# 1/rms of the tokens spread over the partitions by transfers through DRAM, not by products

## The chip, the cores and the metric

One core of a Trainium2 chip (TRN2) runs the whole program in one launch. The metric is the device time of one execution in microseconds (us), the median of the runs shown. Engines: PE (TensorE, matrix products), DVE (VectorE), ACT (ScalarE), POOL (GpSimd), SP (SyncE, which issues most transfers). SBUF is the on-chip memory with 128 partitions, PSUM the one that products write to, in banks.

## The reference

One inference step of a decoder with two layers, on 512 prompt tokens and 8 sample tokens together (520 columns), model width 1024, feed-forward width 2816.

```python
def _rmsnorm(x, g):
    xf = x.astype(jnp.float32)
    y = xf * lax.rsqrt(jnp.mean(xf * xf, axis=-1, keepdims=True) + EPS)
    return (y * g.astype(jnp.float32)).astype(x.dtype)

def _swiglu(x, wg, wu, wd):
    return (jax.nn.silu(x @ wg) * (x @ wu)) @ wd
# every layer:  x += 0.5*SwiGLU(rms(x));  x += mixer(rms(x));  x += 0.5*SwiGLU(rms(x))
# mixer of layer 0: causal pooling over windows of 2, 4, 8, 16; of layer 1: sliding-window
# attention with sinks, on K and V projected once from the stream after layer 0 (_rmsnorm there too)
```

So there is a norm ahead of each of four half layers of SwiGLU, of each mixer, of K and V, and at the end. What matters here is 1/rms, one number for each token.

## The kernel before, in words

The stream is kept turned: model width on the partitions, eight tiles of 128 x 520, tokens along the free dimension. A product is fp32r: each operand is split into a high part (`xh`, `wh`, by ACT) and a low part (`xl`, `wl`, by DVE), and three products of these make one. Feed-forward tiles are made from sums and differences of inputs and of weights (`t12`, `t34`, `th`, `tl`, `S`), so that fewer products do; POOL adds one weight block to another with accumulating transfers (`S<-raw`, `raw<-raw`).

A norm doesn't scale its input. The products run on x times the gain, and 1/rms of each token multiplies the result: `g<-g,R`, `g<-ps,R`, `cs<-cs,R` on DVE. For that, `R` (128 x 520) holds 1/rms of all tokens in every partition. It comes about in two steps. First, sums of squares give 1/rms with the token on the partition, in `r_tok`: four columns for the 512 prompt tokens (token 128 t + p in row p of column t), and a fifth whose rows 112 to 119 hold the sample tokens. Then that is spread: for each column, PE multiplies the identity `ident` by the column broadcast to 128 x 128, which leaves the 128 numbers along the free dimension in all partitions, and ACT copies the bank into `R`. The products are plain fp32, and the profile counts two passes for each, ten for a norm.

This spreading stands at four places:

- place 1: the norm of the first half layer of layer 0 (`first_hooks` calls `rstd_all` between products, about 38 us into the span),
- place 2: the norm of the second half layer of layer 0 (`begin`, steps `N.b`, `N.c0`, `N.c1`, about 412 us),
- place 3: the norm for K and V (the fourth hook of `kv_pass`, about 778 us); the first reader of R here multiplies the cosine and sine tables, `cs<-cs,R`, from which `kT` comes, which PE turns at L1618,
- place 4: the norm of the last half layer (`begin` again, about 1287 us).

At places 1 and 3 `r_tok` is computed by DVE in Newton steps (L506 to L513), at 2 and 4 by POOL with a power (L805). The norms of the pooling mixer, of the attention and the last one have code of their own and aren't touched.

What sets the order: around places 2 and 4 a planner gives each engine its order of steps, from each step's cost and due time (`add(name, engine, cost, due, ...)`); an engine then takes its steps in that order. Elsewhere the order of the program, changed a little by a scheduler, stands. An engine's queue is taken strictly in order: an instruction that waits holds up what is behind it. All weight loads, and every transfer passed through `later(...)`, are issued by SP in the order of the program: `raw<-...gate`, `raw<-...up` (half a megabyte each), `S<-...up` (a quarter).

Of the kernel before, what the change touches and what calls it, by code (L numbers as in the profile page):

```python
# [11 lines left out]
F32 = mybir.dt.float32  # L12
# [6 lines left out]
P = 128  # L19
# [3 lines left out]
SP = 512  # L23
NS = 8
TOK = SP + NS
# [220 lines left out]
class Steps:  # L246
# [8 lines left out]
    def add(self, name, eng, cost, due, fn=None, after=(), takes=(), reads=()):  # L255
        self.steps[name] = (eng, cost, due, fn, tuple(after), tuple(takes))
        for key in reads:
            self.readers.setdefault(key, []).append(name)
# [58 lines left out]
def yoco_step(ctx, tc, ins, outs):  # L317
    nc = tc.nc
# [3 lines left out]
    V, S, T = nc.vector, nc.scalar, nc.tensor  # L322
# [2 lines left out]
    big = ctx.enter_context(tc.tile_pool(name="big", bufs=8))  # L325
    rawp = ctx.enter_context(tc.tile_pool(name="rawp", bufs=3))
    splp = ctx.enter_context(tc.tile_pool(name="splp", bufs=6))
    psum = ctx.enter_context(ExitStack())
    banks_ = []

# [33 lines left out]
    def later(ins):  # L364

        return tc.keep_in_program_order(ins)
# [87 lines left out]
    ident = cp.tile([P, P], F32, name="ident")  # L454
# [14 lines left out]
    r_tok = cp.tile([P, 8], F32, name="r_tok")  # L469
    R = cp.tile([P, TOK], F32, name="R")  # L470
# [18 lines left out]
    pss_ = [None]  # L489
# [22 lines left out]
            o = r_tok[:, :5] if it == 2 else y  # L512
            V.scalar_tensor_tensor(o, t1, 1.5, y, op0=ALU.add, op1=ALU.mult)  # L513

    def rstd_all():

        pr, pr2 = pss_[0][:, 1, :], pss_[0][:, 0, 8 : 8 + NS]
        for t in range(4):
            T.matmul(
                pr[:, t * P : (t + 1) * P], r_tok[:, t : t + 1].broadcast_to([P, P]), ident, start=True, stop=True  # L520
            )
        T.matmul(pr2, r_tok[:, 4:5].broadcast_to([P, P]), ident[:, 112:120], start=True, stop=True)
        S.copy(R[:, :SP], pr)
        S.copy(R[:, SP:], pr2)


    def terms(w, xx):
        return ((w[0], xx[0]), (w[0], xx[1]), (w[1], xx[0]))
# [256 lines left out]
    def begin(st, fi, n, mov, tmp, tt, first, off, base, need, ready, summed, hidden_list, root_):  # L785


        add, vals = st.add, {}
# [15 lines left out]
        def n_root():  # L804
            nc.gpsimd.tensor_tensor(r_tok[:, :5], vals["v"], minus_half, op=ALU.pow)  # L805

        def n_spread():
            pr, pr2 = pss_[0][:, 1, :], pss_[0][:, 0, 8 : 8 + NS]
            for t in range(4):
                T.matmul(  # L810
                    pr[:, t * P : (t + 1) * P], r_tok[:, t : t + 1].broadcast_to([P, P]), ident, start=True, stop=True
                )
            T.matmul(pr2, r_tok[:, 4:5].broadcast_to([P, P]), ident[:, 112:120], start=True, stop=True)

        def n_copy(a):
            if a == 0:
                S.copy(R[:, :SP], pss_[0][:, 1, :])
            else:
                S.copy(R[:, SP:], pss_[0][:, 0, 8 : 8 + NS])

        d = base + root_
        add("N.s", "PE", 0.62, d, n_sums, after=summed, takes=("d",))
        add("N.m", "DVE", 0.17, d, n_mean, after=["N.s"])
        add("N.r", "POOL", 1.4, d, n_root, after=["N.m"])
        add("N.b", "PE", 1.0, d, n_spread, after=["N.r"])
        add("N.c0", "ACT", 0.6, d, lambda: n_copy(0), after=["N.b"])
        add("N.c1", "ACT", 0.18, d, lambda: n_copy(1), after=["N.c0"], reads=[("d", "N.s")])

        def scaled(k, a):
            vals["X", k, a] = z = tmp.tile([P, TOK], F32, tag="sa", name="xab"[:1] + "ab"[a])  # L830
# [23 lines left out]
        for k in range(4):  # L854
            d = S0 - 14.0 + 3.0 * k
# [30 lines left out]
        for p in range(npl):  # L886
# [4 lines left out]
            for q, (k, o) in enumerate(order):  # L891
                i = off + 4 * p + 2 * (k // 4) + o
                after = [f"wl{i}"] + need(k) + ([prev] if prev else [f"p{p - 1}.71"] if p else [])
# [5 lines left out]
            d = P0(p + 1)  # L899
# [4 lines left out]
                reads=[("d", f"p{p}.01"), ("t", f"S{p}")],  # L904
# [103 lines left out]
    with ff_pool() as tmp:  # L1008
# [29 lines left out]
        with tc.tile_pool(name="st", bufs=1, space=bass.MemoryType.PSUM, reuse_waits="tile") as stp:  # L1038
            st = Steps(dict(t=3, m=1, w=6, sq=4))
            add = st.add  # L1040
# [94 lines left out]
            for k in range(KT):  # L1135
                d = T0 + UP * k
                add(
                    f"t{k}", "PE", 0.45, d, lambda k=k: turn_x(k),
                    after=["i"] + [f"x{k // 2}.{c}" for c in range(2)] + ([f"t{k - 1}"] if k else []), takes=("t",),
# [4 lines left out]
                for e, lo, hi, cost in pieces:  # L1144
                    add(
                        f"c{k}{e}", e, cost, d + 0.5, lambda k=k, e=e, lo=lo, hi=hi: copy_x(k, e, lo, hi),
                        after=[f"t{k}"] + (["tab"] if e == "ACT" else []), reads=[("t", f"t{k}")],
# [5 lines left out]
                for o in range(2):  # L1153
# [3 lines left out]
                        after=[f"e{k}", f"wl{w}"] + ([f"p{k - 1}{o}"] if k else []),  # L1157
                        reads=[("w", f"wh{w}")] if k % 4 == 3 else [],
# [5 lines left out]
                    after=[f"q{k}"] + ([f"a{k - 1}"] if k else []), reads=[("sq", f"q{k}")],  # L1164
                )
            for i in range(8):
                d = (6.0, 6.6, 11.5, 12.2, 19.0, 20.5, 22.0, 23.5)[i]
                add(
                    f"wh{i}", "ACT", 0.63, d, lambda i=i: w_hi(i),
                    after=[f"w{i if i < 4 else 7}"] + ([f"wh{i - 1}"] if i else []), takes=("w",),  # L1170
# [104 lines left out]
    with ff_pool() as tmp:  # L1275
# [3 lines left out]
        add = st.add  # L1279
# [165 lines left out]
        for m in (6, 7):  # L1445
            d = 4.35 * (m - 6)
            for h in range(2):
# [13 lines left out]
                after=[f"q{m}", "x5" if m == 6 else "a6"], reads=[("sq", f"q{m}")],  # L1461
# [15 lines left out]
        for gi in range(4):  # L1477
            ready = [f"{k}{2 * gi + i}" for k in ("l", "sl") for i in range(2)] if gi == 3 else ["x5"]
            for tau in (0, 1, 2, 3, 4):
                d = Z_DUE[gi] + 0.72 * tau  # L1480
                add(
                    f"z{gi}{tau}", "PE", 0.71, d + (3.0 if tau == 4 and gi == 0 else 3.5 if tau == 4 and gi == 2 else 0), lambda gi=gi, tau=tau: z_part(gi, tau),
                    after=ready + ([f"z{gi}0"] if tau else []) + (["ns"] if tau == 4 and gi < 2 else [])
# [8 lines left out]
                    after=[f"z{gi}{tau}", "nr" if tau < 4 else "n5"] + ([f"eh{gi}0"] if tau else []),  # L1492
# [5 lines left out]
                    after=[f"eh{gi}{tau}"] + last, reads=[("d", holder)],  # L1498
# [3 lines left out]
        for m in range(KT):  # L1502
            gi, d = m // 2, B_DUE(m)
            need = ((0, 1), (1, 2, 3), (4,))
            for part in range(3):
                add(
                    f"b{m}{part}", "PE", (0.6, 0.72, 0.22)[part], d + 0.1 * part, lambda m=m, part=part: band(m, part),
                    after=[f"ez{gi}{t}" for t in need[part]] + ([f"b{m}0"] if part else [f"b{m - 1}0"] if m else []),
# [4 lines left out]
                reads=[("d", f"b{m}0")],  # L1513
# [6 lines left out]
                reads=[("sq", f"sq{m}")],  # L1520
# [147 lines left out]
    with tc.tile_pool(name="at", bufs=2) as at, tc.tile_pool(  # L1668
        name="pat", bufs=2, space=bass.MemoryType.PSUM, reuse_waits="tile"
# [34 lines left out]
        add = st.add  # L1704
# [191 lines left out]
        for t in range(KT):  # L1896
            d = q_due(t)
# [144 lines left out]
        for g in range(2):  # L2042
            d = S_DUE[g]
# [364 lines left out]
```

## Time and profile before

| what | value |
|---|---|
| median of 3 runs | 1651.93 us (1651.38 to 1654.89) |
| profiled execution | 1651.43 us, span 1649.7 us |
| granted TensorE clock | 0.998 |
| PE, DVE, ACT, POOL busy | 1635.1, 1241.2, 877.0, 178.2 us |
| moved by DMA | 226.28 MB, mean 137 GB/s |
| DMA packets | 317423, of them 9520 under 512 B |

The profile's times are in us from the start of the span. A row of the timeline is: start, duration, engine, line, operation, out<-in, shape, count, and in brackets how long the engine had been idle before and what ended that. Products overlap in the pipeline, so a row's duration is longer than the distance to the next start. "L519" is line 519 of the kernel before. A row of the windows gives, for a stretch of time, the busy time of each engine with its count of instructions, then the granted clock, the mean share of the 16 DMA engines that were busy (it can go a little over 1), and the GB/s that they moved.

### The profile page before, as it was taken

To read this page: it belongs to the slowest core of one execution; us is meant where nothing else is said; L and a number is where in the kernel's file an instruction comes from. 1 tells how busy PE (TensorE), PEld (TensorE's weight loads), DVE (VectorE), ACT (ScalarE), POOL (GpSimd) and SP (SyncE) were. 2 spreads that over 40 slices of the span, in tenths; PEclk is the share of its full clock that TensorE was granted. 3 is DMA by queue.
4 is the path that set the end of the run, shared out by engine and by line. 5 is a ranking of instruction groups with operands and counts; after the bars stand their busy time and mean duration, and the time that the engine had idled before them with its cause. 6 is when DMAs were issued, how large, how long until landed. Compare 5 with 4: busy or idle time off the path is not lost.

```text
span 1649.7 us, 34525 instructions
## 1 busy us (share of the span) xinstructions
PE 1635.1 (99%) x13814; PEld 1620.5 (98%) x13814; DVE 1241.2 (75%) x2351; ACT 877.0 (53%) x1756; POOL 178.2 (11%) x236
## 2 busy tenths in 40 slices
PE   9999999999999999999999999999999999999997
PEld 9999999999999999999999999999989999999997
DVE  7966875878775875878784785778997785785786
ACT  6643643666652652556562552555875662563463
POOL 1101101001101101100201101100220110110100
PEclk9999999999999999999999999999999999999999
DMA  9546845761655765633756665654142566665641
GB/s 244 135 120 136 175 141 137 164 204 54 149 153 134 167 160 135 154 109 97 169 153 155 131 165 152 139 150 114 27 104 65 129 154 166 140 156 149 128 121 52
DMA packets 317423, 226.28 MB, mean 137 GB/s; under 512 B 9520, under 2 KB 292776, under 8 KB 317222
## 3 DMA queue, kind: packets, MB, share of 16 engines
q1 hardware_dynamic: 290832, 178.24, 38.7%
q0 software_dynamic: 23104, 41.31, 15.9%
q10 hardware_dynamic: 3326, 4.53, 0.9%
q8 instruction: 108, 1.77, 0.4%
q14 instruction: 53, 0.43, 0.1%
HBM read 180.63 MB, written 5.04 MB: 113 GB/s over the span
## 4 chain that ended last, share of the span: by engine, by line
PE 97%; DVE 1%; ACT 0%; DMA 0%; issue 0%; SPq 0%; DVEq 0%; ACTq 0%
PE ps L560 48%; PE ps L534 36%; PE pa L534 5%; PE ps L2203 2%; PE ps L1378 1%; PE pb L1808 1%; PE p L534 1%; PE pc L1879 1%; PE pc L1864 1%; PE ps L1415 1%; DMA raw<-in_ffn_w_gate_dram 0%; PE ps L2244 0%; DVE wl L225 0%; PE t L1066 0%; DVE sm L1827 0%; PE ps L498 0%
## 5 line engine op out<-in xcount | busy, mean ns | idle before, releaser
L195 ACT ACTIVATE wh<-raw 128x512 fp32r<-128x512 f32 (+1 forms) x658 | 397.9, 622 | 482.2 <-PE ps L534 285.8
L196 DVE TENSOR_TENSOR wl<-raw,wh 128x512 fp32r<-128x512 f32 (+1 forms) x658 | 434.8, 677 | 176.3 <-ACT wh L195 172.7
L560 PE MATMUL ps<-th,wh 128*128 128x260 f32 x1248 | 352.1, 283 | 1.0 <-DVE sb L653 0.8
L560 PE MATMUL ps<-tl,wh 128*128 128x260 f32 x1248 | 352.4, 282 | 0.0
L560 PE MATMUL ps<-th,wl 128*128 128x260 f32 x1248 | 350.9, 282 | 0.0
L560 PEld LDWEIGHTS ps<-th,wh 128*128 128x128 f32 x1248 | 234.5, 188 | 1.5 <-DVE sb L653 1.0
L560 PEld LDWEIGHTS ps<-tl,wh 128*128 128x128 f32 x1248 | 234.7, 188 | 0.0
L560 PEld LDWEIGHTS ps<-th,wl 128*128 128x128 f32 x1248 | 234.3, 188 | 0.0
L534 PE MATMUL ps<-hh,wh 128*128 128x260 f32 x1024 | 206.5, 283 | 0.6 <-ACT vtok L1630 0.6
L534 PE MATMUL ps<-hl,wh 128*128 128x260 f32 x1024 | 207.0, 282 | 0.0
L534 PE MATMUL ps<-hh,wl 128*128 128x260 f32 x1024 | 205.1, 282 | 0.0
L560 PE MATMUL ps<-xh,wh 128*128 128x260 f32 x696 | 195.0, 282 | 0.6 <-ACT sb L643 0.6
L560 PE MATMUL ps<-xl,wh 128*128 128x260 f32 x696 | 194.9, 282 | 0.0
L560 PE MATMUL ps<-xh,wl 128*128 128x260 f32 x696 | 191.6, 282 | 0.0
L158 POOL DMA_DIRECT2D raw<-raw x78 | 69.2, 887 | 1068.8 <-DVE wl L196 446.0
L534 PEld LDWEIGHTS ps<-hl,wh 128*128 128x128 f32 x1024 | 158.3, 188 | 0.0
L534 PEld LDWEIGHTS ps<-hh,wh 128*128 128x128 f32 x1024 | 157.1, 188 | 0.9 <-ACT vtok L1630 0.9
L534 PEld LDWEIGHTS ps<-hh,wl 128*128 128x128 f32 x1024 | 157.4, 188 | 0.0
L728 DVE TENSOR_TENSOR u<-ps,R 128x520 f32<-128x520 f32 x86 | 60.0, 698 | 98.0 <-PE ps L534 98.0
L560 PEld LDWEIGHTS ps<-xh,wh 128*128 128x128 f32 x696 | 130.8, 188 | 0.8 <-ACT sb L643 0.8
L560 PEld LDWEIGHTS ps<-xl,wh 128*128 128x128 f32 x696 | 131.1, 188 | 0.0
L534 PE MATMUL ps<-xl,wh 128*128 128x260 f32 x640 | 130.2, 283 | 0.0
(339 smaller groups left out, 3297.2 us busy)
## 6 DMA issues: line engine op xcount, KB each, us to landing
raw<-in_ffn_w_gate_dram SPq DMA_DIRECT2D x87, 512.0 KB
raw<-in_ffn_w_up_dram SPq DMA_DIRECT2D x87, 512.0 KB
raw<-in_ffn_w_down_dram SPq DMA_DIRECT2D x32, 1024.0 KB
S<-in_ffn_w_up_dram SPq DMA_DIRECT2D x78, 256.0 KB
raw<-raw POOLq DMA_DIRECT2D x78, 256.0 KB, 3.4
S<-raw POOLq DMA_DIRECT2D x78, 256.0 KB, 4.8
raw<-in_ffn_w_down_dram SPq DMA_DIRECT2D x16, 768.0 KB
raw<-in_w_q_dram SPq DMA_DIRECT2D x8, 512.0 KB
```

Of the source, the lines that this page charges most:

```text
L158: G.dma_start(blk(raw, 2, 1), blk(raw, 1, 1), accum_op=ALU.add)
L195: nc.scalar.activation(dh, src, AF.Copy)
L196: nc.vector.tensor_tensor(dl, src, dh.bitcast(F32), op=ALU.subtract)
L534: T.matmul(banks[:, hf, :H], a[:, kk, :], hcols(b, hf), start=(first and i == 0), stop=(last and i == 2),)
L560: T.matmul(bank[:, :H], a[:, kk, :], b, start=(not more and kk == 0 and i == 0), stop=(kk == 3 and i == 2), skip_group_check=more,)
L728: V.tensor_tensor(halves(u), banks[m][:, :, :H], halves(R), op=ALU.mult)
L1378: T.matmul(o, a[:, s], b[:, kk, :], start=(n == 0), stop=(n == 5))
L1415: T.matmul(o, za, b, start=(i == 0), stop=(i == len(lst) - 1))
L1808: T.matmul(o, q_[rows_, qc], k_[rows_, kc_], start=(i == 0), stop=(i == 2))
L1864: T.transpose(pt[:, o : o + P], vals["sm", t, h, bi][:, e, kt * P : (kt + 1) * P], ident)
L1879: T.matmul(po[rows_, bi * P : (bi + 1) * P], vtok[:, max(b - 1, 0) + kt, v0 : v0 + 64], vals["pp", t, h, bi][:, kt * 256 + e * P : kt * 25 ...
L2203: T.matmul(bank, a[:, k % 3, :], b[:, c0:c1], start=(k == 0 and i == 0), stop=(k == 5 and i == 2))
```

## The change

Two tiles in DRAM of 1 x 520 are added (`drp`, two buffers). At each of the four places SP now issues three transfers: four columns of `r_tok` to 512 places of the row (128 x 4 single elements), the eight sample tokens to the last eight places, and the row, read once for every partition, into `R`. The third waits until the other two have landed. The ten passes on PE and the two copies on ACT are gone. The planner is told 4.5 us of transfer where it had 1.0 us of PE, and the PSUM bank with the sums is given back after the mean (`N.m`) and not after the copy.

```diff
+    drp = ctx.enter_context(tc.tile_pool(name="drp", bufs=2, space=bass.MemoryType.DRAM))
...
-    def rstd_all():
-
-        pr, pr2 = pss_[0][:, 1, :], pss_[0][:, 0, 8 : 8 + NS]
-        for t in range(4):
-            T.matmul(
-                pr[:, t * P : (t + 1) * P], r_tok[:, t : t + 1].broadcast_to([P, P]), ident, start=True, stop=True
-            )
-        T.matmul(pr2, r_tok[:, 4:5].broadcast_to([P, P]), ident[:, 112:120], start=True, stop=True)
-        S.copy(R[:, :SP], pr)
-        S.copy(R[:, SP:], pr2)
-
+    def spread():
+
+        row = drp.tile([1, TOK], F32, name="row")
+        cols = row[0:1, :SP].rearrange("o (t p) -> p (o t)", p=P)
+        later(nc.sync.dma_start(cols, r_tok[:, :4]))
+        later(nc.sync.dma_start(row[0:1, SP:].rearrange("o p -> p o"), r_tok[112:120, 4:5]))
+        later(nc.sync.dma_start(R, row[0:1, :].broadcast_to([P, TOK])))
+
+    rstd_all = spread
...
         d = base + root_
         add("N.s", "PE", 0.62, d, n_sums, after=summed, takes=("d",))
-        add("N.m", "DVE", 0.17, d, n_mean, after=["N.s"])
+        add("N.m", "DVE", 0.17, d, n_mean, after=["N.s"], reads=[("d", "N.s")])
         add("N.r", "POOL", 1.4, d, n_root, after=["N.m"])
-        add("N.b", "PE", 1.0, d, n_spread, after=["N.r"])
-        add("N.c0", "ACT", 0.6, d, lambda: n_copy(0), after=["N.b"])
-        add("N.c1", "ACT", 0.18, d, lambda: n_copy(1), after=["N.c0"], reads=[("d", "N.s")])
+        add("N.b", "dma", 4.5, d, spread, after=["N.r"])
+        add("N.c1", "-", 0.0, d, after=["N.b"])
```

`n_spread` and `n_copy`, which did in `begin` what `rstd_all` did elsewhere, go too. In the orders below names end in a running number, which differs between the two programs, and the changed kernel's lines are numbered anew (L1187 is L1171 there, L875 is L859, L1559 is L1543).

SP at place 1, before: the last weight loads of the burst at 32 to 37 us, and the next chunk.

```order
L372 DMA raw5_575<-in_ffn_w_gate_dram 128x8x128
L372 DMA raw5_575<-in_ffn_w_up_dram 128x8x128
L372 DMA S_578<-in_ffn_w_up_dram 128x4x128
L372 DMA S_817<-in_ffn_w_up_dram 128x4x128
L372 DMA raw6_872<-in_ffn_w_gate_dram 128x8x128
```

SP at place 1 with the change.

```order
L373 DMA raw5_577<-in_ffn_w_gate_dram 128x8x128
L373 DMA raw5_577<-in_ffn_w_up_dram 128x8x128
L373 DMA S_580<-in_ffn_w_up_dram 128x4x128
L520 DMA row_608<-r_tok_89 128x4x1
L521 DMA row_608<-r_tok_89 8x1
L522 DMA R_90<-row_608 128x520
L373 DMA S_816<-in_ffn_w_up_dram 128x4x128
L373 DMA raw6_871<-in_ffn_w_gate_dram 128x8x128
```

The three transfers stand between the two S loads; the second S load is now behind R. In the same way they stand ahead of the loads of raw38 at place 2, of raw72 at place 3 and of raw116 at place 4.

DVE at place 2, before: from the last inputs of a tile to the first gate (`g_5561`), its use and its low part (`hl_5616`).

```order
L845 SCALAR_TENSOR_TENSOR t34_5548<-t12_5529,xb_5527 128x260
L875 TENSOR_TENSOR g_5561<-ps95_5358,R_88 128x520
L225 TENSOR_TENSOR wl_5559<-raw36_4796,wh_5558 128x512
L852 TENSOR_TENSOR tl_5570<-t12_5529,th_5569 128x520
L882 SCALAR_TENSOR_TENSOR g_5561<-ps96_5369,t_5583 128x520
L225 TENSOR_TENSOR wl_5597<-raw36_4796,wh_5596 128x512
L852 TENSOR_TENSOR tl_5538<-t34_5494,th_5537 128x520
```

The same stretch of DVE with the change.

```order
L829 SCALAR_TENSOR_TENSOR t34_5560<-t12_5532,xb_5530 128x260
L225 TENSOR_TENSOR wl_5552<-raw36_4795,wh_5551 128x512
L836 TENSOR_TENSOR tl_5563<-t12_5532,th_5562 128x520
L836 TENSOR_TENSOR tl_5542<-t34_5493,th_5541 128x520
L859 TENSOR_TENSOR g_5608<-ps95_5357,R_90 128x520
L225 TENSOR_TENSOR wl_5591<-raw36_4795,wh_5590 128x512
```

The gate moved behind one low part of weights and two of inputs.

DVE at place 3, before: the second half of the rotation of K (`kT`), with what stands around it.

```order
L1558 TENSOR_TENSOR rp1_10108<-rp1_10108,cs_9951 128x520
L196 TENSOR_TENSOR wl_10350<-raw71_9904,wh_10349 128x512
L1612 TENSOR_TENSOR vT_10303<-ps167_10114,R_88 128x520
L1612 TENSOR_TENSOR vT_10304<-ps168_10115,R_88 128x520
L1559 TENSOR_TENSOR kT0_9939<-kT0_9939,rp1_10101 128x520
L1559 TENSOR_TENSOR kT1_9940<-kT1_9940,rp1_10108 128x520
```

The same stretch of DVE with the change.

```order
L1542 TENSOR_TENSOR rp1_10101<-rp1_10101,cs_9947 128x520
L1596 TENSOR_TENSOR vT_10296<-ps167_10107,R_90 128x520
L1596 TENSOR_TENSOR vT_10297<-ps168_10108,R_90 128x520
L196 TENSOR_TENSOR wl_10399<-raw71_9900,wh_10398 128x512
L680 TENSOR_TENSOR t34_10335<-xb_10331,xa_10330 128x260
L1543 TENSOR_TENSOR kT0_9935<-kT0_9935,rp1_10094 128x520
L1543 TENSOR_TENSOR kT1_9936<-kT1_9936,rp1_10101 128x520
```

The two sums that finish `kT` moved behind a low part of weights and a difference of inputs.

At place 1 DVE's order up to `g<-g,R` is the same as before; right behind it a low part of weights changed places with a low part of inputs, and between `g<-g,R` and the tl that PE takes at 55.83 us stand the same operations.

More of the change, by code (lines that the diff above doesn't have):

```diff
@@ L805, in n_root @@
             nc.gpsimd.tensor_tensor(r_tok[:, :5], vals["v"], minus_half, op=ALU.pow)
[L807 to L819, printed above, removed]
         d = base + root_
         add("N.s", "PE", 0.62, d, n_sums, after=summed, takes=("d",))
-        add("N.m", "DVE", 0.17, d, n_mean, after=["N.s"])
+        add("N.m", "DVE", 0.17, d, n_mean, after=["N.s"], reads=[("d", "N.s")])
         add("N.r", "POOL", 1.4, d, n_root, after=["N.m"])
-        add("N.b", "PE", 1.0, d, n_spread, after=["N.r"])
-        add("N.c0", "ACT", 0.6, d, lambda: n_copy(0), after=["N.b"])
-        add("N.c1", "ACT", 0.18, d, lambda: n_copy(1), after=["N.c0"], reads=[("d", "N.s")])
+        add("N.b", "dma", 4.5, d, spread, after=["N.r"])
+        add("N.c1", "-", 0.0, d, after=["N.b"])
         def scaled(k, a):
```

## The prediction, made before the changed kernel ran

> **What bounds the kernel now.** I read the totals first, then the chain of work that ended last, then what TensorE (PE) waits for.
>
> ```profile
> PE 1635.1 (99%) x13814; PEld 1620.5 (98%) x13814; DVE 1241.2 (75%) x2351; ACT 877.0 (53%) x1756; POOL 178.2 (11%) x236
> PE 97%; DVE 1%; ACT 0%; DMA 0%; issue 0%; SPq 0%; DVEq 0%; ACTq 0%
> ```
>
> ```profile
> PE ps L2244 <- ACT xg L2232: 2.0, 2, 1.0
> ...
> PE ps L560 <- ACT wh L195: 0.2, 1, 0.2
> ```
>
> PE is busy for 99% of the span and is 97% of the chain. The eleven rows of its waits, of which the first and the last stand here, sum to 7.6 us. So a PE instruction that goes is time saved, as long as nothing makes PE wait in its place, and a new PE wait is time lost. Everything else in the change counts only through that.
>
> **What it removes.** Each place gives up its products and the two copies on ScalarE (ACT). What they cost PE is the distance from the first of them to the next ordinary product.
>
> ```profile
> 38.88 1.05 PE L519 MATMUL ps<-ident,r_tok 128*128 128x128 f32 x8
> ...
> 39.92 0.37 PE L534 MATMUL ps<-xl,wh 128*128 128x260 f32 x1
> ```
>
> ```profile
> 412.93 1.05 PE L810 MATMUL ps<-ident,r_tok 128*128 128x128 f32 x8
> ...
> 413.96 0.48 PE L534 MATMUL ps<-xh,wh 128*128 128x260 f32 x2
> ```
>
> ```profile
> 778.90 1.05 PE L519 MATMUL ps<-ident,r_tok 128*128 128x128 f32 x8
> ...
> 779.94 0.37 PE L534 MATMUL ps<-hh,wh 128*128 128x260 f32 x1
> ```
>
> ```profile
> 1287.02 0.40 PE L534 MATMUL ps<-xh,wl 128*128 128x260 f32 x2
> 1287.37 1.16 PE L810 MATMUL ps<-ident,r_tok 128*128 128x128 f32 x8
> ...
> 1288.50 0.48 PE L534 MATMUL ps<-xh,wh 128*128 128x260 f32 x2
> ```
>
> That is 1.04, 1.03 and 1.04 us. At place 4 products start about every 0.12 us, so the two that start at 1287.02 leave PE free near 1287.26, and the distance to 1288.50 is 1.24 us with some waiting in it. All together: 4.35 us, or 0.26% of the time. Nothing else is removed from PE, so this bounds the gain. (About 0.2%, 3.3 us, is what a measurement of this kernel can tell from no change.) ACT's copies lie beside PE's work and count for nothing.
>
> **What a spreading by transfers takes.** No row shows 4-byte writes. The nearest are these: the two hardware and software queues, and a store from SBUF to DRAM in quiet rings.
>
> ```profile
> q1 hardware_dynamic: 290832, 178.24, 38.7%
> q0 software_dynamic: 23104, 41.31, 15.9%
> ```
>
> ```profile
> out_dram<-hrow POOLq DMA_DIRECT2D x2, 16.0 KB, 1.8
> ```
>
> A packet of q1, on which the new transfers go, took 0.387 x 1649.7 x 16 / 290832 = 0.035 us of one engine; one of q0 took 0.159 x 1649.7 x 16 / 23104 = 0.182 us. The first new transfer writes 512 single elements. If they spread over 16 engines, 32 on each, they take 1.1 us by q1's packets and 5.8 us by q0's. I take 1.1, since it is the same queue, and keep 5.8 as the bad end; a packet of 4 bytes could in principle be cheaper than q1's mean of some 613 bytes, which would save less than 1 us. With the 1.8 us from issue to landing, the row in DRAM is complete 2.9 us after 1/rms is known. Only then can SP issue the third transfer: 1.8 us and 266 KB (128 x 520 x 4 bytes), 0.9 us at the 299 GB/s of the row 37:38 below. In quiet rings R is there 5.6 us after r_tok; in the rows below its first reader started 3.1 to 5.8 us after r_tok.
>
> **Place 1, the first norm.** The rows are, in order: SP's queue, VectorE (DVE) making r_tok and first using R, the DMA share by microsecond (last two columns), then DVE results and the products that take them.
>
> ```profile
> 34.38 2.75 SPq L372 DMA_DIRECT2D S<-in_ffn_w_up_dram  x2
> ```
>
> ```profile
> 36.32 0.16 DVE L513 SCALAR_TENSOR_TENSOR r_tok<-nt,ny 128x5 f32<-128x5 f32 x1
> ...
> 41.12 0.69 DVE L1187 TENSOR_TENSOR g<-g,R 128x520 f32<-128x520 f32 x1
> ...
> 49.97 0.69 DVE L617 TENSOR_TENSOR g<-ps,R 128x520 f32<-128x520 f32 x1
> ...
> 53.41 0.68 DVE L196 TENSOR_TENSOR wl<-raw,wh 128x512 fp32r<-128x512 f32 x1
> ...
> 54.35 0.69 DVE L359 TENSOR_TENSOR tl<-t,th 128x520 fp32r<-128x520 f32 x1
> ...
> 59.99 0.69 DVE L196 TENSOR_TENSOR wl<-raw,wh 128x512 fp32r<-128x512 f32 x1 [1.08 <-ACT wh L195]
> ```
>
> ```profile
> 37.00:38.00 1.00, 1.00 (x11) 1.00 (x10) 0.90 (x2) 1.00 (x2) 0.61 (x1) 1.00 1.22 299
> ...
> 40.00:41.00 1.00, 1.00 (x10) 1.00 (x10) 1.00 (x3) 0.65 (x2) 0.30 (x1) 1.00 1.07 207
> 41.00:42.00 1.00, 1.00 (x11) 1.00 (x10) 1.00 (x3) 0.76 (x2) 1.00 (x2) 1.00 0.21 41
> 42.00:43.00 1.00, 1.00 (x11) 1.00 (x9) 1.00 (x3) 1.00 (x2) 0.96 (x2) 1.00 1.04 178
> ```
>
> ```profile
> 53.07 0.28 PE L560 MATMUL ps<-xh,wh 128*128 128x260 f32 x1
> ...
> 54.62 0.28 PE L560 MATMUL ps<-xh,wl 128*128 128x260 f32 x1
> ...
> 55.83 0.28 PE L560 MATMUL ps<-tl,wh 128*128 128x260 f32 x1
> ```
>
> r_tok is ready at 36.48, in the middle of a burst of weight loads that keeps the rings full until about 41.1. The first of the two S loads now stands ahead of the row write on SP, the second behind R. Taking the second out (262 KB at 299 GB/s, 0.9 us), the rings reach the row's elements at about 40.2 us. Their 1.1 us and a tail of some 0.4 (a guess) put the row's landing at 41.7. R then takes 1.8 us and 266 KB beside POOL's accumulating transfers, at the 178 GB/s of 42:43 1.5 us: R lands at 45.0. DVE wants it at 41.12, with no cover: g<-g,R stands tenth behind r_tok in its row, and behind it wait the low parts of weights and inputs that PE needs. So DVE stands still for 3.9 us.
>
> Does PE feel it? Up to 59.99 DVE's rows have no idle time of note, so the delay isn't made up on the way. g at 49.97 ends at 50.66 and frees the bank of the products at 53.07, a lead of 2.4 us; wl ends at 54.09 for 54.62, a lead of 0.5; tl ends at 55.04 for 55.83, 0.8. The same rows stand between r_tok and tl as before; wl moves ahead of one 0.6 us operation, so its lead is about 1.1, and tl's 0.8 is the least. Against the old times PE loses 3.9 - 0.8 = **+3.1 us**, and the 1.04 us that it is early there is inside that figure. Ends: +0.8, where the row passes beside the loads (36.48 + 2.9 + 3.3 = 42.7, DVE late by 1.6), and +7.8, with 5.8 us of writing.
>
> [...]
>
> The second S load comes some 5 us late. POOL adds it into a sum that PE wants only a tile later, so I cost it at nothing; with that cover gone it would count from there on.
>
> **Place 2, the second half layer.** The rows: POOL's root, the first use of R, and the product whose bank that use frees.
>
> ```profile
> 410.48 1.25 POOL L805 TENSOR_TENSOR r_tok<-nv,minus_half 128x5 f32<-128x5 f32 x1 [12.94 <-DVE nv L802]
> ```
>
> ```profile
> 414.83 0.70 DVE L875 TENSOR_TENSOR g<-ps,R 128x520 f32<-128x520 f32 x1 [0.65 <-ACT R L819]
> ```
>
> ```profile
> 423.42 0.40 PE L534 MATMUL ps<-xh,wh 128*128 128x260 f32 x2
> ```
>
> R at 411.73 + 5.6 = 417.3, 2.5 us later than before. The planner now puts three operations (a wl, two tl) ahead of the g that needs R, and PE wants that bank at 423.42 - 1.03. Hidden, with 4 us to spare: **-1.03**. The loads of raw38 and of its S stand behind R and come 3 to 4 us later; POOL's sums on them feed the tile after next. Cover gone, either lateness would count in full.
>
> **Place 3, the norm ahead of K and V.**
>
> ```profile
> 774.08 0.37 SPq L372 DMA_DIRECT2D raw<-in_ffn_w_gate_dram  x1
> ```
>
> ```profile
> 775.92 0.17 DVE L513 SCALAR_TENSOR_TENSOR r_tok<-nt,ny 128x5 f32<-128x5 f32 x1
> ...
> 780.80 1.31 DVE L1606 TENSOR_TENSOR cs<-cs,R 128x520 f32<-128x520 f32 x2
> ...
> 786.90 1.30 DVE L1559 TENSOR_TENSOR kT<-kT,rp 128x520 f32<-128x520 f32 x2
> ```
>
> ```profile
> 790.41 0.27 PE L1618 MATMUL ps<-ident,kT 128*128 128x128 f32 x1
> ```
>
> ```profile
> 787.79 0.63 ACT L195 ACTIVATE wh<-raw 128x512 fp32r<-128x512 f32 x1 [1.32 <-PE ps L534]
> ```
>
> The load of 774.08 (raw72) now stands behind R on SP, so the rings are quiet: R at 776.09 + 5.6 = 781.7, DVE late by 0.9. The kT sums, at 786.90, are now behind a wl and a t as well, 1.0 us: the first ends at 787.6 + 1.9 = 789.5, and PE, early by 1.04, would turn kT at 789.37. It waits 0.1 to 0.2: **-0.9**. raw72 is issued 5 us late, near 779; a megabyte at 299 GB/s is 3.5 us, so it is there near 784.5, ahead of ACT's 787.79.
>
> **Place 4, the last half layer.**
>
> ```profile
> 1285.08 2.23 POOL L805 TENSOR_TENSOR r_tok<-nv,minus_half 128x5 f32<-128x5 f32 x1
> ```
>
> ```profile
> 1293.10 0.70 DVE L875 TENSOR_TENSOR g<-ps,R 128x520 f32<-128x520 f32 x1 [1.19 <-PE ps L534]
> ```
>
> R at 1287.31 + 5.6 = 1292.9, and before the change R's first reader already waited for PE until 1293.10. No loss: **-1.24**.
>
> **The sum.** +3.1 - 1.03 - 0.9 - 1.24 = -0.1 us. The planner also puts the steps of both planned stretches into another order; I cost that at nothing, within 1 us either way, as the whole program has only 7.6 us of PE waits to win or to repeat. The profiled execution took 1651.43 us (span 1649.7 and 1.73 around it), 0.50 below the median of the runs, 1651.93. On the median's scale the forecast is **1651.8 us**.
>
> **The rivals.** *Slower: 4-byte writes are dear.* Every 1 us more for the row costs 1 us at place 1 and 1 us at place 3, where the cover is already used up; at 2 and 4 it is free for some 4 us. +3.3 us is reached when the row's writing takes 2.8 us and not 1.1, that is 88 ns an element and engine, well inside 35 to 182. At 4 us the time is 1651.8 + 2 x 2.9 = 1657.6; at 5.8 it is 1661.2. For it: nothing on q1 shows less than whole rows of hundreds of bytes. Against it: q0's dear packets also add in place, which these don't. [...]
>
> *Faster: R is early or its wait hidden at place 1.* That needs R by 41.9, so a row that has landed by about 39, 2.5 us after r_tok and straight through full rings. Then all four places gain: 1651.9 - 4.3 = 1647.6. With the row merely beside the loads (+0.8) it is 1649.5, still within the band.
>
> *Loads held by SP.* SP stands in R's wait for 3 to 5 us at each place. If raw72 is read at place 3 before it has landed, ACT and then PE wait; from the rows it has 3 us to spare, so this only adds to the slow case.
>
> **How the numbers follow.** No change to be told: 0.55 (place 1 eats the gain of the others; its own range is 1649.0 to 1655.0). Slower by over 0.2%: 0.32 (the dear writes, mostly; place 1's delay has no cover, and every error in the row's landing goes straight to PE). Faster: 0.13. The range of 8 in 10 leaves out the fully hidden case and the upper end of the writes: 1648.6 to 1659.0.
>
> **What would show it.** Right, if g<-g,R at 41 us starts near 45 after an idle time of about 4 us that ends with a DMA on R, PE waits 2 to 4 us in all at about 52 to 58 us at L559, and places 2 and 4 show no PE wait; about 2,000 more packets under 512 B. Wrong, if DVE's wait at 41 us is under 1 us, or R comes later than 6 us after r_tok at places 2 to 4, where the rings are quiet: there the price of the row's writes can be read alone.

## The result, and the profile after

The changed kernel takes 1692.99 us (1691.01 to 1694.22, 4 runs) against 1651.66 us (1651.32 to 1654.89) of the kernel before beside it: 1.025 times as long, 95% interval 1.0237 to 1.0262. The profiled execution took 1693.79 us with a span of 1692.0, 42.3 us more than the span of before. Forecast was no change that could be told, 1651.8 us with a range up to 1659.0.

The totals, the chain and the longest waits of PE, as they were read before (busy time and share, then share of the chain; then us in total, how often, the longest):

```profile
PE 1646.0 (97%) x13774; PEld 1627.7 (96%) x13774; DVE 1240.3 (73%) x2351; ACT 875.9 (52%) x1748; POOL 178.1 (11%) x236
PE 89%; DMA 5%; DVE 4%; ACT 1%; issue 1%; POOL 0%; SPq 0%; DVEq 0%; POOLq 0%; ACTq 0%
```

```profile
PE ps L1602 <- DVE kT L1543: 9.0, 1, 9.0
PE ps L559 <- ACT sa L922: 3.9, 2, 2.7
PE ps L559 <- ACT g L1172: 3.7, 1, 3.7
PE ps L533 <- DVE g L859: 3.4, 1, 3.4
PE ps L559 <- ACT wh L195: 3.3, 1, 3.3
PE ps L1640 <- DVE acc L488: 2.6, 1, 2.6
```

PE has 40 instructions fewer (13814 to 13774: four times ten) and yet is busy 10.9 us longer, and its waits sum to 38.6 us (all 23 rows) where they were 7.6. 31.0 of waits and 10.9 of busy time make 41.9 of the 42.3 us. The passes that went were 4.3 us of busy time (1.05 three times and 1.16, in the rows of before), so the products that are left take 15.2 us longer. So there are two things to find: what PE waits for, and why the same products take longer.

SP's queue answers the first. Columns: start, duration of the issue, what is issued. Places 1 to 4 in order:

```profile
36.99 0.81 SPq L520 DMA_DIRECT2D row<-r_tok  x1
37.85 0.58 SPq L521 DMA_DIRECT2D row<-r_tok  x1
48.06 0.35 SPq L522 DMA_DIRECT2D R<-row  x1
...
423.73 0.37 SPq L520 DMA_DIRECT2D row<-r_tok  x1
424.14 0.41 SPq L521 DMA_DIRECT2D row<-r_tok  x1
433.35 0.34 SPq L522 DMA_DIRECT2D R<-row  x1
433.79 0.38 SPq L373 DMA_DIRECT2D raw<-in_ffn_w_gate_dram  x1
...
799.49 0.37 SPq L520 DMA_DIRECT2D row<-r_tok  x1
...
809.73 0.34 SPq L522 DMA_DIRECT2D R<-row  x1
...
1324.96 0.37 SPq L520 DMA_DIRECT2D row<-r_tok  x1
...
1333.12 0.34 SPq L522 DMA_DIRECT2D R<-row  x1
```

The third transfer waits until the row has landed: SP issues nothing from 424.55 to 433.35 at place 2, and raw's load 0.4 us behind R. R is issued 9.6, 10.2 and 8.2 us after the first at places 2, 3 and 4, in rings that are nearly empty (a DMA share of 0.00 ahead of the write at places 2 and 3; at place 4 after the first 1.5 us), and 11.1 us after it at place 1. Forecast was 2.9. On DVE the first reader of R then starts (the bracket says how long DVE had been idle, and what ended it):

```profile
52.10 0.70 DVE L1171 TENSOR_TENSOR g<-g,R 128x520 f32<-128x520 f32 x1 [10.68 <-DMA R<-row]
...
438.47 0.70 DVE L859 TENSOR_TENSOR g<-ps,R 128x520 f32<-128x520 f32 x1 [10.49 <-DMA R<-row]
...
814.20 1.31 DVE L1590 TENSOR_TENSOR cs<-cs,R 128x520 f32<-128x520 f32 x2 [10.16 <-DMA R<-row]
...
1337.45 0.70 DVE L859 TENSOR_TENSOR g<-ps,R 128x520 f32<-128x520 f32 x1 [7.98 <-DMA R<-row]
```

That is 4.0 to 5.1 us after R's issue, forecast 2.7 in quiet rings. From r_tok to R it takes 12.5 to 15.4 us and not 5.6.

What stood behind R on SP came late in its turn. At place 2 the chain of work that ended last goes on like this (start, duration, what):

```profile
434.88 8.01 DMA S<-in_ffn_w_up_dram
...
443.58 8.00 DMA S<-raw
...
451.66 0.64 ACT wh L221
```

The chain runs on from there to PE's wait of 2.7 us at 461.

While the row is on its way, the DMA engines show almost nothing. The windows (last two columns: mean busy share of 16 engines, GB/s):

```profile
424.00:425.00 1.00, 1.00 (x10) 1.00 (x10) 1.00 (x3) 1.00 (x3) 0.00 (x0) 1.00 0.25 2
425.00:426.00 1.00, 1.00 (x11) 1.00 (x10) 1.00 (x4) 1.00 (x3) 0.00 (x0) 1.00 0.01 0
...
428.00:429.00 1.00, 1.00 (x11) 1.00 (x10) 0.00 (x0) 0.44 (x1) 0.00 (x0) 1.00 0.00 0
```

A quarter of one microsecond on 16 engines is 4 engine-microseconds for about 520 pieces, by estimate some 8 ns each; R, which waits for them, is issued 8 us later.

The second thing is the granted clock (the third column from the right) beside the count of products in brackets behind PE's busy time:

```profile
64.00:66.00 2.00, 2.00 (x11) 2.00 (x11) 2.00 (x5) 1.08 (x2) 0.00 (x0) 0.50 0.00 0
...
70.00:72.00 2.00, 2.00 (x18) 2.00 (x19) 0.95 (x2) 1.13 (x3) 0.00 (x0) 1.00 0.14 36
```

After some of PE's pauses the clock stands at 0.50 for 3 to 8 us of work, and in two microseconds of full work PE starts 11 products and not 18 or 19. These are the first products after four of the pauses (the bracket has the pause):

```profile
53.56 0.56 PE L559 MATMUL ps<-xh,wh 128*128 128x260 f32 x1 [3.69 <-ACT g L1172]
...
62.54 0.58 PE L559 MATMUL ps<-xh,wh 128*128 128x260 f32 x1 [3.30 <-ACT wh L195]
...
439.31 0.48 PE L533 MATMUL ps<-xh,wh 128*128 128x260 f32 x2 [3.43 <-DVE g L859]
...
460.95 0.58 PE L559 MATMUL ps<-th,wh 128*128 128x260 f32 x1 [2.73 <-ACT sa L922]
```

The low clock came with the first, the second and the fourth (there at 458 us, when two pauses of 1.6 and 1.5 us lay just behind), and not with the third; it also came with the 9.0 us at place 3 and the 2.6 us for `acc` at 1153 us. Summed over the two-microsecond windows with a clock under 1, busy time times what the clock lacks, this is 5.3 us after place 1, 2.0 after place 2, 3.8 after place 3 and nothing after place 4. Two more stretches stand at no place: 3.3 us at 6 to 16 us, ahead of place 1, and 1.7 us at 1154 to 1158 us. All together that is 16.1 us, where the products take 15.2 us longer. But the 3.3 are no time lost against the kernel before: there PE starts as few products in 8 to 12 us (6 and 11 for 8 and 12), with the clock shown at 1.00, and r_tok is made only 0.2 us later with the change. The other 12.8 are most of the 15.2; where the rest lies isn't shown.

By where the same point of the program stands in both traces (the start of r_tok or of the mean ahead of it), place 1 cost 11.8 us, place 2 11.4, place 3 15.5 and place 4 3.4. (One expectation below counts place 4 from the end of POOL's r_tok, which took 2.23 us before and 1.33 with the change, and so gives 14.3 and 4.7 for the last two.) Of the 15.5 us between places 3 and 4, 11.2 have come by 1131 us (the `g<-sa,ps` that starts at 1096.71 before starts at 1131.32). The other 4.3 come at 1151 to 1158 us, in the attention, where PE waits 2.6 us for `acc` and the low clock follows. Nothing of the change stands there. A wait at this point, of 1.9 to 4.0 us, is also in five of the versions below (those with 16-byte pieces, with 128 pieces, with 64 and with 16 bytes between pieces, and the one on POOL) and not in the other seven; how it comes from the change isn't shown.

### The profile page after: what moved, and what is told of

Read it like the earlier page. It is cut to its first block, busy times and chain, and to the rows that moved or that the text cites. A ratio compares the mean times of both kernels' runs of the same rounds, so it can differ in the third digit from the quotient of the medians.

```text
span 1692.0 us, 34459 instructions
## 1 busy us (share of the span) xinstructions
PE 1646.0 (97%) x13774; PEld 1627.7 (96%) x13774; DVE 1240.3 (73%) x2351; ACT 875.9 (52%) x1748; POOL 178.1 (11%) x236
## 4 chain that ended last, share of the span: by engine, by line
PE 89%; DMA 5%; DVE 4%; ACT 1%; issue 1%; POOL 0%; SPq 0%; DVEq 0%; POOLq 0%; ACTq 0%
PE ps L559 45%; PE ps L533 31%; PE pa L533 5%; PE ps L2187 2%; DMA row<-r_tok 2%; DMA S<-raw 1%; PE ps L1362 1%; PE p L533 1%; DMA S<-in_ffn_w_up_dram 1%; PE pb L1792 1%; PE pc L1863 1%; PE pc L1848 1%; DMA R<-row 1%; PE ps L1399 1%; DMA raw<-in_ffn_w_up_dram 0%
## 5 line engine op out<-in xcount | busy, mean ns | idle before, releaser
L559 PE MATMUL ps<-xh,wh 128*128 128x260 f32 x696 | 196.8, 285 | 7.5 <-ACT g L1172 3.7
L559 PE MATMUL ps<-xl,wh 128*128 128x260 f32 x696 | 196.2, 284 | 0.0
L533 PE MATMUL ps<-xh,wh 128*128 128x260 f32 x640 | 130.1, 285 | 3.4 <-DVE g L859 3.4
```

Source lines behind the costliest of these rows:

```text
L533: T.matmul(banks[:, hf, :H], a[:, kk, :], hcols(b, hf), start=(first and i == 0), stop=(last and i == 2),)
L559: T.matmul(bank[:, :H], a[:, kk, :], b, start=(not more and kk == 0 and i == 0), stop=(kk == 3 and i == 2), skip_group_check=more,)
```

## The experiments

Each expectation stands as it was recorded before the run. "The row takes" means from the issue of the first transfer to that of the third.

**Pieces of 16 bytes.** The row is laid out by partition, so that the four columns of a partition are one piece.

```diff
-        cols = row[0:1, :SP].rearrange("o (t p) -> p (o t)", p=P)
+        cols = row[0:1, :SP].rearrange("o (p t) -> p (o t)", t=4)
```

> The row in DRAM is laid out with the four columns of a token's partition side by side, so the first write is 128 pieces of 16 bytes in place of 512 of 4 (R then holds the right numbers at the wrong tokens). In the changed kernel the third transfer was issued 9.6 us after the first at place 2, 10.2 at place 3. Theory A (the price is the number of pieces written, some 16 to 18 ns each, one after another): 3 to 4.5 us. Rival B (any small store to DRAM from SP's queue takes that long to be reported): 9 to 10 us. Rival C (pieces that share a stretch of DRAM get in each other's way): 3 to 5 us, as a stretch of 64 bytes is touched 4 times and not 16.

```profile
419.04 0.34 SPq L520 DMA_DIRECT2D row<-r_tok  x1
419.43 0.34 SPq L521 DMA_DIRECT2D row<-r_tok  x1
420.70 0.33 SPq L522 DMA_DIRECT2D R<-row  x1
```

1.66 us at place 2, 1.65 at place 3 and 2.4 at place 4, where the rings are full for the first microsecond; 1669.36 us in one run. A fixed price of 9 to 10 us, as in B, falls. Faster than A and C both said. The eight sample tokens (the second row) are still single adjoining elements here, and R was issued 1.3 us after them: eight of these cost little.

**A quarter of the pieces, side by side.**

```diff
-        later(nc.sync.dma_start(cols, r_tok[:, :4]))
+        later(nc.sync.dma_start(flat[0:1, :P].rearrange("o p -> p o"), r_tok[:, :1]))
```

> Only one column of 128 tokens is written, 128 pieces of 4 bytes that lie side by side; R's other tokens get a constant. Theory A (number of pieces): third transfer issued 3 to 4.5 us after the first at places 2 and 3. Rival B (fixed): 9 to 10. Rival C (pieces in the same 64 bytes): still 16 to a stretch, so 7 to 10 if that is what takes the time.

```profile
423.32 0.34 SPq L522 DMA_DIRECT2D far<-r_tok  x1
423.71 0.34 SPq L523 DMA_DIRECT2D far<-r_tok  x1
430.40 0.33 SPq L524 DMA_DIRECT2D R<-far  x1
```

7.1 us, 7.5 at place 3, 6.6 at place 4; 1689.49 us in one run. With 128 pieces, as many as in the first experiment, but of 4 bytes and adjoining, most of the delay is there; a quarter of the pieces saves 1.5 to 2.7 us. The number of pieces (A) isn't what most of it is paid for.

**All 512 pieces, 64 bytes apart.**

```diff
-        cols = row[0:1, :SP].rearrange("o (t p) -> p (o t)", p=P)
+        cols = flat[0:1, : SP * 16].rearrange("o (t p s) -> p (o t) s", p=P, s=16)[:, :, 0]
```

> 512 pieces of 4 bytes again, but each 64 bytes from the next in DRAM; R reads the same 2080 bytes as before, so most of its numbers are a constant. Theory A (number of pieces): third transfer 8 to 10 us after the first, as in the changed kernel. Rival B (fixed): the same 9 to 10. Rival C (shared stretches): 2 to 4 us.

```profile
418.21 0.37 SPq L523 DMA_DIRECT2D far<-r_tok  x1
418.62 0.41 SPq L524 DMA_DIRECT2D far<-r_tok  x1
420.47 0.34 SPq L525 DMA_DIRECT2D R<-far  x1
```

2.3 us, 2.0 at place 3, 1.9 at place 4; 1668.34 us in one run. The same number of 4-byte writes, and the delay is gone. That is as theory C had it: the delay came with pieces that lie close together in DRAM (9.6 us at place 2 for adjoining ones). What in the memory or on the way to it makes them late isn't shown.

**16 bytes apart** (the same with 4 for 16).

> 512 pieces of 4 bytes again, each 16 bytes from the next in DRAM, so that a stretch of 64 bytes is touched 4 times, not 16 (as in the changed kernel) and not once (64 bytes apart, where the third transfer came 2.0 to 2.3 us after the first). Theory C (pieces in one stretch of DRAM follow one another): 2.3 to 4 us. If the size of a piece against its distance mattered (a 4-byte write into a stretch that others write, however few): 7 to 10 us.

```profile
418.81 0.37 SPq L523 DMA_DIRECT2D far<-r_tok  x1
419.22 0.41 SPq L524 DMA_DIRECT2D far<-r_tok  x1
421.32 0.34 SPq L525 DMA_DIRECT2D R<-far  x1
```

2.5 us, 2.6 at place 3, 2.7 at place 4; 1670.39 us in one run. Four pieces in 64 bytes cost 0.25 to 0.8 us more than one; sixteen, in the changed kernel, cost 6.3 to 8.3 more. Distances between 4 and 16 bytes weren't tried, so how close is too close stays open.

**Turned by PE, written as whole rows.** One product turns r_tok, ACT copies 5 x 128.

```diff
+    def r_turn():
+        T.transpose(pss_[0][:5, 1, :P], r_tok[:, :5], ident)
+    def r_turned():
+        S.copy(rt, pss_[0][:5, 1, :P])
...
-        later(nc.sync.dma_start(cols, r_tok[:, :4]))
-        later(nc.sync.dma_start(row[0:1, SP:].rearrange("o p -> p o"), r_tok[112:120, 4:5]))
+        later(nc.sync.dma_start(row[0:1, :SP].rearrange("o (t p) -> (o t) p", p=P), rt[:4, :]))
+        later(nc.sync.dma_start(row[0:1, SP:], rt[4:5, 112:120]))
```

> PE turns r_tok (one product in two passes instead of ten), ACT copies 5 x 128 to SBUF, and the row is written as whole pieces of 512 bytes; all else as in the changed kernel, SP's order included. Theory A and C: the row is there 2 to 3 us after its issue, R about 7 us after r_tok; waits of PE at places 2 and 4 go, places 1 and 3 keep 2 to 5 us each: 1653 to 1662 us in all. Rival B (any small store): 9 to 10 us for the row and a total of about 1690.

```profile
417.04 0.29 SPq L527 DMA_DIRECT2D row<-rt  x1
417.38 0.24 SPq L528 DMA_DIRECT2D row<-rt  x1
418.48 0.35 SPq L529 DMA_DIRECT2D R<-row  x1
```

The row takes 1.4 to 1.5 us at places 2 to 4; R's reader starts 4.0 us after R's issue at place 2 and 4.6 at place 3. 1664.95 us, ratio 1.0088 (1.0063 to 1.0113): two thirds of the loss are gone with the row's writing, and the total is some 3 us above what was expected. The largest waits of PE were for high parts of weights (4.0 us in two), for kT (2.7) and for a copy by ACT (2.7).

**The same, issued by ACT.**

```diff
-        later(nc.sync.dma_start(R, row[0:1, :].broadcast_to([P, TOK])))
+        later(nc.scalar.dma_start(R, row[0:1, :].broadcast_to([P, TOK])))
```

(and so for the two writes).

> As the version that turns r_tok and writes whole rows (1664.95 us), but the three transfers are issued by ACT, so no weight load on SP stands behind R. Theory (held loads cost some us at places 2 and 3): 1656 to 1661. Rival (in that version SP stands for only 1.5 us, so the loads hardly matter, and ACT now stands in the wait): 1664 to 1670.

1657.42 us (7 runs), ratio 1.0036 (1.0021 to 1.0050). No weight load stands behind R now, and 7.5 us are gone from the total though SP had stood for only 1.5 us. In its profiled execution (1654.96 us), which reached place 1 1.9 us earlier, place 2 gains 1.0 us on the kernel before, places 1 and 3 lose 2.8 us each and place 4 loses 0.8. PE's largest wait for R's readers, at place 3, and one at place 1:

```profile
PE ps L1615 <- DVE kT L1556: 2.2, 2, 1.9
...
PE ps L570 <- ACT sa L651: 1.5, 1, 1.5
```

**R from 128 different rows.** On the version that turns r_tok.

```diff
-        later(nc.sync.dma_start(R, row[0:1, :].broadcast_to([P, TOK])))
+        later(nc.sync.dma_start(R, wide))
```

> As the version that turns r_tok, but R is read from 128 rows that lie one after another in DRAM (266 KB, the first of them the new row, the others a constant), not 128 times from one row of 2080 bytes. In that version R came 4.0 to 4.6 us after its issue, where 2.7 had been forecast. Theory A (all engines reading the same 2 KB get in each other's way): 2.5 to 3.2 us at places 2 and 3. Rival (266 KB beside the weight loads just behind it on the queue take that long): still 4.0 to 4.6.

```profile
791.52 0.35 SPq L534 DMA_DIRECT2D R<-wide  x1
```

```profile
794.31 1.31 DVE L1608 TENSOR_TENSOR cs<-cs,R 128x520 f32<-128x520 f32 x2 [1.43 <-DMA R<-wide]
```

2.8 us from issue to reader at place 3, with the same bytes and the same loads behind; from one row it was 4.6 in the version that it was made from. At place 2 R came before DVE wanted it. At place 3, with one run each, reading one row 128 times costs 1.8 us. (1666.85 us in one run; at place 1 the row was written only at 44.9 us there, so this time isn't compared.)

**Issued by POOL**, otherwise as the changed kernel.

```diff
-        later(nc.sync.dma_start(cols, r_tok[:, :4]))
+        later(nc.gpsimd.dma_start(cols, r_tok[:, :4]))
```

(and so for the other two).

> The changed kernel with the three transfers issued by POOL on its software queue, so that no weight load on SP stands behind R; POOL's own accumulating transfers now stand behind it. Theory (the row is late because its 4-byte pieces share stretches of DRAM, whatever the queue): R is issued 7 to 11 us after the row here too. Rival (SP's hardware queue is what is slow with single elements): 2 to 4 us. On the held loads: in the changed kernel place 2 cost 11.3 us, and its waits at 453 to 461 us were for sums on weights whose loads stood behind R. With SP free they come earlier, and 5 to 8 us of that go: 1683 to 1690. Rival: POOL holds the sums up just as long, 1691 to 1696.

```profile
421.11 0.84 POOL L520 DMA_DIRECT2D row<-r_tok  x1 [0.29 <-POOL r_tok L804]
421.95 0.53 POOL L521 DMA_DIRECT2D row<-r_tok  x1
431.79 0.58 POOL L522 DMA_DIRECT2D R<-row  x1 [9.30 <-DMA row<-r_tok]
```

10.7 us, 9.3 at place 3, where SP's queue had 9.6 and 10.2: the queue isn't the cause. 1683.96 us, ratio 1.0193 (1.0171 to 1.0214), 9 us less than the changed kernel. Place 2 cost 8.0 us for 11.4: its later waits are gone, but R took 7.3 us from POOL's issue to its reader, and PE waited 7.0 for it.

**The planner told 14 us.**

```diff
-        add("N.b", "dma", 4.5, d, spread, after=["N.r"])
+        add("N.b", "dma", 14.0, d, spread, after=["N.r"])
```

> The changed kernel with one number changed: the planner is told 14.0 us for the transfers, not 4.5, which moves the first use of R 17 rows back in DVE's order at place 2 and 16 at place 4. Theory A (places 2 and 4 pay mostly because DVE and PE stand in a wait that was planned too short): PE's 3.4 us wait for g at place 2 and most of place 4's loss go, 1680 to 1686. Rival (what they pay for is the weight loads held behind R on SP): place 2's waits for sums and weights at 453 to 461 us stay and the time stays within 1689 to 1694.

DVE and PE at place 2:

```profile
450.54 0.69 DVE L225 TENSOR_TENSOR wl<-S,wh 128x512 fp32r<-128x512 f32 x1 [15.39 <-ACT wh L221]
```

```profile
453.89 0.77 PE L533 MATMUL ps<-xh,wh 128*128 128x260 f32 x2 [17.69 <-DVE g L859]
```

1695.11 us, ratio 1.0263 (1.0246 to 1.0281): nothing gained. DVE no longer waits for R at place 2. It waits 15.4 us for S, whose load stands behind R on SP, and the g that frees PE's bank now stands behind that in DVE's row. From place 4 to the end only 0.2 us are lost now and not 3.4. So the plan mattered at place 4, the held loads at place 2, which costs 18.2 us here and not 11.4.

**Products at places 1 and 3, transfers at 2 and 4** (`rstd_all` as in the kernel before).

> Transfers at places 2 and 4 only, the ten passes at 1 and 3 as before. In the changed kernel's trace the end moved by 12.0, 11.3, 14.3 and 4.7 us at the four places. Theory (each place pays for itself): +16.0, about 1667. Rival (place 2 pays because of loads that place 1 made late, and so on): clearly less, below 1660.

1668.86 us, ratio 1.0103 (1.0086 to 1.0120), +17.5 us. In its profile place 2 cost 11.2 us and place 4 4.1, near the 11.4 and 3.4 of the changed kernel: each place's loss is nearly its own.

**Filling PE's pause, twice.** To see what the low clock costs, PE was to get useless work into the 9.0 us at place 3.

```diff
             pk = ps()
+            for _ in range(36):
+                T.matmul(pk[:, :P], ident, ident, start=True, stop=True)
```

> The changed kernel, and at place 3 PE gets 36 products of the identity with itself (72 passes, 8 to 9 us) just ahead of the point where it waited 9.0 us for kT; their result is overwritten. Theory (a pause makes the granted clock fall to 0.5, and the products after it run at half speed for some 8 us): the clock stays at 1.00 at place 3, and although PE does 8 to 9 us more work the whole is about 4 us shorter, 1689. Rival (the low clock is only how idleness is recorded): no change or up to 1 us longer, 1693 to 1694.

1702.14 us, ratio 1.0297 (1.0278 to 1.0317). The bank for the useless products came free only with a reader of R, so they stood behind a pause of 7.3 us and were paid in full. The second try put 28 of them ahead of PE's last products:

```diff
         vb = kv_pass(during_v)
+        for _ in range(28):
+            T.matmul(vb[1][:, 0, 384:512], ident, ident, start=True, stop=True)
```

> The first try at this put PE's useless products behind the wait and not into it. Now 28 products of the identity with itself (56 passes, 6.3 us at full clock) come ahead of PE's last products before kT at place 3, so that PE gets to its wait 6.3 us later and the wait of 9.0 us shrinks to about 3. Theory (the long pause makes the granted clock fall): the clock stays at 1.00 after it, the products there no longer run at half speed, and the whole is 3 to 4 us shorter than the changed kernel's 1693, about 1689, though PE does more. Rival (the low reading costs nothing): 1692 to 1694.

1695.71 us, ratio 1.0269 (1.0252 to 1.0286). PE's other products moved too, the pause was still 7.1 us, and the clock fell to 0.50 in it, as before. Neither run tells the theories apart; that the clock costs time rests on the counts of products above (11 for 18 or 19 in 2 us).

## Why the prediction was wrong, step by step

**The step that failed is the price of the row's writes.** It was put at 1.1 us from q1's 35 ns a packet, with 5.8 from q0's as the bad end. The row took 8.2 to 10.2 us from issue to landing in quiet rings; less the 1.8 that were about right for a small store (1.4 with whole rows), that is 6.4 to 8.4, beyond the bad end. Both rows that bounded it were of transfers with large pieces, 613 bytes a packet on q1 and 1788 on q0. The price isn't one of an element and an engine: the engines were done in about a microsecond (a share of 0.25 in 424 to 425, 0.01 in the next), 512 pieces 64 bytes apart took 1.9 to 2.3 us, and 128 adjoining ones took 6.6 to 7.5. A bound taken from the mean of other traffic didn't hold the one thing that was new, adjoining 4-byte writes.

The slower rival pointed to this side. The runs draw it narrower: small pieces alone were cheap, 1.9 to 2.3 us for 512 of 4 bytes at 64 bytes apart and 2.5 to 2.7 at 16; adjoining ones took 8.2 to 10.2.

That q1 shows nothing below hundreds of bytes was misread: SP's sixteen loads of the sinks (`sink_s`) are 0.1 KB each; but they are loads, and no bound for a write. For the landing the prediction took the quietest row. The same list of before has a store of 8 KB that took 8.1 us (`out_dram<-knew`, behind other transfers of POOL), so that term too had a wider range in its rows than it was given.

**This step is not all of it.** With the pieces 64 bytes apart the time was still 1668.34 us, 17.7 us above the kernel before beside it and outside the range. So the dear writes are some 24 of the 41 us, and terms that the prediction had short or at nothing are the rest: R's transfer, the loads behind R, the clock, and the wait in the attention. How the rest divides among them isn't shown.

**R's transfer** was put at 2.7 us and took 4.0 to 5.1. At place 3, from 128 rows and not from one, it is 2.8 for 4.6, so most of this miss there is that all partitions read the same 2080 bytes.

**The loads behind R** were costed at nothing at place 2, with the warning that either lateness would count with the cover gone. SP stood for 8.8 us, where the loads were to come 3 to 4 us late, and the cover was gone: the sums on raw38 and S came late, PE waited 2.7 us and less at 453 to 461, and with the plan mended it waited 17.7. Even 1.5 us of standing was not free (1.0088 against 1.0036, though with the queue other things changed too).

**The clock** was no term of the sum. In the profile of before it reads under 1 only behind PE's last product (0.67 and 0.50 from 1644 us on), and PE's longest wait was 1.1 us. With the change the clock fell to 0.50 with the pauses of 3.7 and 3.3 us at place 1, of 9.0 at place 3, and after several in a row (the last of 1.6 and 1.5) at place 2. It came back after 3 to 8 us of work. A pause of 3.4 us at 439 us left it at 1.00, where 3.7 at 53 us, 3.3 at 62 and 2.6 at 1153 came with 0.50; and at 7 us it fell with no pause over 0.8 us behind PE's first product. What sets it here is more than the length of one pause, and stays open.

**Place by place.** Place 1: +3.1 forecast, +11.8 measured; the mechanism was as described (DVE stands at g<-g,R without cover, PE follows), but DVE stood for 10.7 us and not 3.9, and the low clock came on top (7.4 us of PE's waits, 5.3 of clock, less the 1.04 that went). That the row would wait behind SP's own loads in the full rings was an estimate, and its size was right: with pieces 64 or 16 bytes apart R was issued 4.9 us after r_tok there (1.9 to 2.7 us after the first write at places 2 to 4), where the forecast had the row landed after 5.2. In what order the rings took the row and the loads isn't shown. Place 2: -1.03, measured +11.4; in the version with whole rows on ACT's queue it came to -1.0, so the cover of 4 us was there for a wait of the size forecast. Place 3: -0.9, measured +11.2 and the 4.3 in the attention; kT was the wait named, 9.0 us for 0.1 to 0.2. Place 4: -1.24, measured +3.4 (0.2 with 14 us in the plan). The removed passes were right: 40 instructions, and no place gained more than they took. The packets under 512 B rose by 2240, where about 2,000 were forecast.

**The rivals.** The slower one, with 0.32, named the right step, the landing of the 4-byte writes. Its mechanism was half right: 512 writes of 4 bytes weren't dear 16 or 64 bytes apart (1.9 to 2.7 us), adjoining ones were (8.2 to 10.2). Its size was wrong: it counted each microsecond once at places 1 and 3 and took 2 and 4 as covered, and ended at 1661.2. What the adjoining writes alone cost is the distance to the runs without them (one each), 1693 to between 1668 and 1670, some 23 to 25 us.

## What to carry to other kernels

A way through DRAM costs two landings one after the other (here 9.6 us for the row and 5.1 for R at place 2), and what it is worth hangs on how long a landing takes in just that shape: where no row of the trace shows such a write, its price is open upwards, and the range must say so, above all on a path without cover. Don't scatter adjoining single elements into DRAM: write whole rows, or turn the data first (1.4 us for 9.6 at place 2). Even so, no version tried here was faster than the ten passes of PE: the best took 1.0036 times as long. And a transfer that waits, put on a queue kept in order, holds the loads behind it (SP stood for 8.8 us at place 2, with the loads of raw38 and S behind R); it belongs on a queue where nothing urgent stands.

## What the runs showed of the hardware that was not expected

- Adjoining 4-byte writes to DRAM (places 2 to 4): 128 of them took 6.6 to 7.5 us to land, 512 took 8.2 to 10.2; 512 of them 16 bytes apart took 2.5 to 2.7, 64 bytes apart 1.9 to 2.3; 128 pieces of 16 bytes 1.7 to 2.4. The same from SP's and from POOL's queue (9.3 to 10.7). The DMA engines look idle meanwhile (a share of 0.00 in 428 to 429 us).
- A row of 2080 bytes in DRAM read 128 times took 1.8 us longer than 128 rows of that size (4.6 us for 2.8 from issue to reader, place 3, one run each).
- Half the clock with pauses of PE of 2.6 to 9.0 us, at 458 us after two of 1.6 and 1.5, and at 7 us with none over 0.8, for 3 to 8 us of work once PE resumed; one pause of 3.4 us left it at full. At 8 to 12 us of the kernel before PE started as few products (6 and 11 in two microseconds) with the clock shown at 1.00.
